# An encoder on one core: adds moved from Pool to VectorE, another start of an operand ring, and the times of four tiles

## The chip, the cores and the metric

The kernel runs on one core of a Trainium2 chip. The metric is device time in microseconds (us) for one execution. The core's engines each work through their own instructions in order: TensorE (PE in the profile, with PEld for its weight loads), VectorE (DVE), ScalarE (ACT), Pool (POOL, also called GpSimd) and SP, which only issues DMA transfers here. An engine that waits for a semaphore holds everything behind it on that engine.

## The reference

Two layers of an encoder over 1024 tokens of 1024 numbers, all in float32. Each layer adds a mixer and then a gated feed-forward block (FFN) to the stream:

```python
for l in range(DEPTH):                       # 2
    h = _rmsnorm(x, g_pre_mix[l])
    z = h @ w_in[l]                          # Fourier, windowed and memory groups
    ...
    x = x + _rmsnorm(y @ w_out[l], g_post_mix[l])   # y: the three groups, each normed
    h = _rmsnorm(x, g_pre_ffn[l])
    gate, up = jnp.split(h @ w_ffn_in[l], 2, axis=-1)
    f = (jax.nn.silu(gate) * up) @ w_ffn_out[l]     # D_FF = 2816
    x = x + _rmsnorm(f, g_post_ffn[l])
```

## The kernel before

**Tiles and precision.** The tokens are 8 tiles of 128 rows; tiles 0 to 3 are one half, 4 to 7 the other. Every float32 matmul is made from two rounded parts of each operand: `split` (L151, L152) writes the high part by a cast on ScalarE and the low part by a subtraction, mostly on VectorE, and three matmuls take hi*hi, hi*lo and lo*hi.

**The FFN.** Both FFN matrices are multiplied by a scheme with 7 products instead of 8 on 2 x 2 blocks. Each product takes sums or differences of blocks, so that there are many adds of 128 x 512 beside the matmuls.
- *Mixer to w_ffn_in.* `Mix.out` makes the mixer's output of a tile (eviction L1041), scales it and adds it to the stream (`residual`, L337 and L338), and norms it (`norm_x`, L294; its scale is computed in L210 and L212). `Blocks.tile` transposes the normed tile (L1066) and copies it to SBUF (L1067), and `Blocks.sum` and `Blocks.last` add the halves (L1084, L1096, L1097) into the operands that w_ffn_in's products share.
- *w_ffn_in.* `Quad.step` does the seven products of one block column in the order 2, 4, 5, 1, 6, 7, 3 (L1137). Its weights are loaded on SP (L1112), summed on VectorE (L1127) and split. 11 steps do all of gate and up. At the end of each, `up_out` multiplies (L1189), forms the sums that w_ffn_out's products need (L1199 to L1203) and writes them to `actd` in DRAM (L1193).
- *w_ffn_out.* `ffn_out` goes through the products 5, 3, 4, 1, 7, 2, 6 over 11 steps k. In each step `out_sums` loads an activation block from `actd` (L1233) and one or two weight blocks (L1239), adds these two (L1251; products 2 and 5 have none), on VectorE for even k and on Pool for odd k, and splits both into an operand of the ring `abs_`; 12 matmuls follow (L1270). At the end of a product the PSUM tiles are added into four result blocks (L1294 to L1309); for product 4 Pool does L1301.
- *The results of a tile.* `last_x` loads a tile of the stream (L1426), `last_tile` scales and adds: in layer 0 by `residual` (L337, L338) and back to DRAM (L1436), in layer 1 by `residual_out` (L327, L328) with half of the row stored from SP and half from ScalarE's queue (L329). Tiles 0 to 3 have their place inside the last two products, tiles 4 to 7 behind the last.

**Order and memory.** Nearly all buffers are places in one arena, handed out by rings, each with a list of slots that it goes round. Ring `abs_` is reset at each layer's w_ffn_out. The blocks of w_ffn_in's operands lie in slots too: block 2 in 64 and 72, block 4 in 80 and 88; `qws`, the raw weights, goes through 44, 48, 52, 56 from the second step. `zf_load`, for layer 1's mixer, writes its operands to slots 64 to 80 and is called behind product 1. The order of the instructions on each engine isn't that of the code: a scheduler with a model of the engines decides it when the program is built, so a change of one engine shifts others.

Of the kernel before, what the change touches and what calls it, by code (L numbers as in the profile page):

```python
# [16 lines left out]
ALU = mybir.AluOpType  # L17
# [5 lines left out]
NT = S // P  # L23
# [10 lines left out]
NFF = DFF // P  # L34
# [34 lines left out]
def tile_encoder(ctx: ExitStack, tc: tile.TileContext, T, C, out):  # L69
    nc = tc.nc  # L70
# [65 lines left out]
    wcs, abs_ = Ring(112, 116, 96, 100, 48, 52, 56, 60), Ring(80)  # L136
# [183 lines left out]
    def residual_out(x, f, g, dst, t):  # L320

        ss = sm(1, "rss")
        nc.scalar.activation(junks(D // 2).bitcast(BF16), f, AF.Square, accum_out=ss)
        r = rsqrt_mean(ss, D, 1, "rrs")
        for n in range(2):
            ns = slice(n * 512, n * 512 + 512)
            nc.vector.scalar_tensor_tensor(out=f[:, ns], in0=f[:, ns], scalar=r[:, 0:1], in1=g[:, ns], op0=ALU.mult, op1=ALU.mult)  # L327
            (nc.gpsimd if t in (1, 3, 5) else nc.vector).tensor_tensor(out=x[:, ns], in0=x[:, ns], in1=f[:, ns], op=ALU.add)  # L328
            (nc.sync, nc.scalar)[n].dma_start(dst[:, ns], x[:, ns])  # L329

    def residual(x, f, g, eng=None):
# [154 lines left out]
    class Mix:  # L486
# [543 lines left out]
        def out(self, t, x1):  # L1030

            x, f = self.xf.pop(t)
            (hi, lo), rs = self.prepped.pop(t)
            for n in range(2):
                ns = slice(n * 512, n * 512 + 512)
                pt = ps([512], "mo")
                acc = Acc(pt, 4)
                for i in range(4):
                    w = self.woa[2 + i]
                    acc.add(hi[:, i], lo[:, i], w[0][:, ns], w[1][:, ns])  # L1040
                nc.vector.scalar_tensor_tensor(  # L1041
                    out=f[:, ns], in0=pt, scalar=rs[:, 0:1], in1=f[:, ns], op0=ALU.mult, op1=ALU.add
                )
            residual(x, f, self.gpost, nc.gpsimd if t < NT - 1 else nc.vector)
            return norm_x(x, self.gffn, f, x1)


# [2 lines left out]
    class Blocks:  # L1050
# [18 lines left out]
        def sum(self, i, c, lo_eng=None):  # L1069

            b11, b21 = self.raw[0, 0], self.raw[0, 1]
            if i not in (2, 4):
                b12, b22 = self.raw[1, 0], self.raw[1, 1]
            sl = slice(c * P, c * P + P)
            if i not in self.b:
                self.b[i] = [big(4, 512) if k is None else at(k, 4, 512, dt=F32R) for k in self.HB[i]]
            if i == 2:
                s = b11[:, :, sl]
            if i == 5:
                s = b22[:, :, sl]  # L1080
            if i in (1, 4, 6):
                s = sums(4, P)
                x, y, op = (b21, b11, ALU.subtract) if i == 4 else (b11, b22 if i == 1 else b12, ALU.add)
                (nc.gpsimd if i == 6 else nc.vector).tensor_tensor(out=s, in0=x[:, :, sl], in1=y[:, :, sl], op=op)  # L1084
            if i == 7:
                s = b21[:, :, sl]
            if i == 3:
                s = b12[:, :, sl]
            hi, lo = (b[:, :, sl] for b in self.b[i])
            split(hi, lo, s, lo_eng)  # L1090

        def last(self, c):

            sl = slice(c * P, c * P + P)
            b12, b21, b22 = (self.raw[k][:, :, sl] for k in ((1, 0), (0, 1), (1, 1)))
            nc.gpsimd.tensor_tensor(out=b21, in0=b21, in1=b22, op=ALU.add)  # L1096
            nc.vector.tensor_tensor(out=b12, in0=b12, in1=b22, op=ALU.subtract)  # L1097

    ORDER = (2, 4, 5, 1, 6, 7, 3)
# [83 lines left out]

    def up_out(q, g, actd, p):

        V, G = nc.vector, nc.gpsimd
        a = [acts(512) for _ in range(4)]
        for i, c in enumerate(q.out):
            (G if i in (0, 3) else V).tensor_tensor(out=a[i], in0=c, in1=g[i], op=ALU.mult)  # L1189
        a11, a21, a12, a22 = a  # L1190

        def put(i, s):
            nc.sync.dma_start(actd[i - 1, p], s)  # L1193

        put(3, a11)
        put(4, a22)
        for i, x, y, eng in ((1, a11, a22, G), (2, a21, a22, V), (5, a11, a12, G)):
            s = acts(512)
            eng.tensor_tensor(out=s, in0=x, in1=y, op=ALU.add)  # L1199
            put(i, s)  # L1200
        V.tensor_tensor(out=a21, in0=a11, in1=a21, op=ALU.subtract)
        put(6, a21)
        G.tensor_tensor(out=a12, in0=a12, in1=a22, op=ALU.subtract)  # L1203
        put(7, a12)
# [24 lines left out]
    def out_sums(l, actd, i, k):  # L1229

        ab = abs_(2, 2, 512, dt=F32R)
        raw = ras(512)
        lastld[0] = nc.sync.dma_start(raw, actd[i - 1, k])  # L1233
        split(ab[:, 0, 0], ab[:, 0, 1], raw)

        def block(r, c):
            w = rbs(512)
            r0 = (2 * k + r) * P
            nc.sync.dma_start(w, T["w_ffn_out"][l, r0 : r0 + P, c * 512 : c * 512 + 512])  # L1239
            return w  # L1240

        if i in (2, 5):
            s = block(i == 5, i == 5)
        else:
            x, y, op = {
                4: ((1, 0), (0, 0), ALU.subtract), 3: ((0, 1), (1, 1), ALU.subtract), 1: ((0, 0), (1, 1), ALU.add),
                7: ((1, 0), (1, 1), ALU.add), 6: ((0, 0), (0, 1), ALU.add),
            }[i]
            x, y = block(*x), block(*y)
            s = bsums(512)  # L1250
            (nc.vector, nc.gpsimd)[k % 2].tensor_tensor(out=s, in0=x, in1=y, op=op)  # L1251
        split(ab[:, 1, 0], ab[:, 1, 1], s)
        return ab

    def ffn_out(l, actd, load, out, after, half, late):
# [16 lines left out]
        for i in (5, 3, 4, 1, 7, 2, 6):  # L1272
# [5 lines left out]
            for k in range(n):  # L1278
                ops.append(out_sums(l, actd, i, k))
                for p in range(whole):  # L1280
                    step(pts[p], p, ops[k], k == 0, k == n - 1, new)
                t = {(2, 2): 0, (2, 7): 1, (6, 1): 2, (6, 5): 3}.get((i, k))
                if t is not None:
                    load(t)
                    out(t, rows[t])
                if i == 6 and k in (7, 8, 9, 10):
                    load(k - 3)
            for p in range(4):
# [9 lines left out]
                    TT(out=c22[p], in0=pt, in1=c22[p], op=sub)  # L1298
                if i == 4:
                    nc.scalar.copy(c21[p], pt)  # L1300
                    nc.gpsimd.tensor_tensor(out=c11[p], in0=c21[p], in1=c11[p], op=sub)  # L1301
                if i == 1:
                    TT(out=c22[p], in0=pt, in1=c22[p], op=add)
                if i == 7:
# [53 lines left out]
    for l in range(DEPTH):  # L1358
# [69 lines left out]
        def last_tile(t, f):  # L1428
# [3 lines left out]
            if l == DEPTH - 1:  # L1432
                residual_out(x, f, st["gpf"], x_out[t], t)
                return
            residual(x, f, st["gpf"], nc.gpsimd if t < NT - 1 else None)
            nc.sync.dma_start(x2d[t], x)  # L1436
            token_scale(x, t)
            st[t] = x
# [2 lines left out]

        last = l + 1 == DEPTH
        abs_.i = 0
        abs_.ks = (64, 72, 80, 88, 16, 24, 0, 8, 32, 40, 48, 56, 96, 104, 112) if last else (80, 88, 48, 56, 96, 104)

        def after(i):
            if last:
                return
            if i == 5:
                mem.make()  # L1450
            if i == 1:
                mix.zf_load()
                mix.fourier_tables(28)
# [48 lines left out]
```

## Time and profile before

| | |
|---|---|
| times of three runs | 2122.41, 2131.86, 2132.92 us |
| median | 2131.86 us |
| the profiled execution | 2126.91 us |
| its span | 2125.1 us |
| granted TensorE clock, mean | 0.974 |
| TensorE busy | 2005.6 us (94%) |
| VectorE / ScalarE / Pool busy | 1572.2 / 1069.6 / 880.9 us |

The profile is that of one execution. Times in it start with the span; a row of the timeline has the start, the time to its end, the engine, the line, the operation, its output and inputs, their sizes, a count of like instructions put together, and in brackets how long the engine had been idle before and what released it. Layer 0's mixer ends at about 388 us, its w_ffn_in at about 837, its w_ffn_out at about 1050; layer 1's at about 1440, 1891 and the end.

### The profile page before, as it was taken

How to read it: one execution, taken by the hardware profiler on the slowest of the kernel's cores; microseconds unless marked ns; L12 is line 12 of the kernel's file. 1: busy time of each engine (PE TensorE's matmuls, PEld its weight loads, DVE VectorE, ACT ScalarE, POOL GpSimd, SP SyncE). 2: the span in 40 equal slices, each digit the busy share in tenths (PEclk: the TensorE clock that was granted, in tenths of full speed). 3: DMA queues.
4: the chain of work that ended last, by engine and by line, in shares of the span. 5: the costliest groups of instructions: out<-in, count | busy, mean ns of one | idle time of the engine just before them, and what ended most of it. 6: DMA issues, size and time to landing. Idle time of an engine off the chain costs nothing.

```text
span 2125.1 us, 28571 instructions
## 1 busy us (share of the span) xinstructions
PE 2005.6 (94%) x9587; PEld 1654.4 (78%) x9587; DVE 1572.2 (74%) x2429; ACT 1069.6 (50%) x2270; POOL 880.9 (41%) x922
## 2 busy tenths in 40 slices
PE   7998999699999999999899979996999999989997
PEld 6886877488888887788788768775888888878785
DVE  5668756897877877667847686679987787877774
ACT  7567777543333334454545676675433333345441
POOL 5344438533434335331634544574442333432222
PEclk9998999899999999999999989998999999999998
DMA  6112223422323326888821122142232232379882
GB/s 219 44 45 65 71 89 119 139 75 92 122 94 105 109 88 222 276 275 268 282 84 47 44 70 97 68 139 99 85 130 94 95 112 91 124 232 324 290 277 90
DMA packets 173347, 286.48 MB, mean 135 GB/s; under 512 B 15464, under 2 KB 73360, under 8 KB 173200
## 3 DMA queue, kind: packets, MB, share of 16 engines
q1 hardware_dynamic: 165136, 265.78, 38.0%
q10 hardware_dynamic: 8064, 18.88, 2.3%
q8 instruction: 75, 1.23, 0.2%
q14 instruction: 72, 0.59, 0.1%
HBM read 218.02 MB, written 66.58 MB: 134 GB/s over the span
## 4 chain that ended last, share of the span: by engine, by line
PE 75%; DVE 8%; DMA 5%; ACT 4%; POOL 4%; issue 3%; SPq 0%; POOLq 0%; DVEq 0%; ACTq 0%
PE fo L1270 14%; PE qy L1137 11%; PE qz L1137 11%; PE qx L1137 11%; PE mo L162 6%; PE qw L1137 5%; PE kvp L162 4%; DVE arena_r L152 3%; PE qp L162 3%; PE zT L162 2%; DMA arena_f<-in_w_ffn_out 2%; DMA arena_f<-actd 2%; PE pT L798 1%; ACT arena_r L151 1%; PE sc L761 1%
## 5 line engine op out<-in xcount | busy, mean ns | idle before, releaser
L151 ACT CAST arena_r<-arena_f 128x512 fp32r<-128x512 f32 (+2 forms) x780 | 443.3, 591 | 673.0 <-PE qz L1137 115.2
L152 DVE TENSOR_TENSOR arena_r<-arena_f,arena_r 128x512 fp32r<-128x512 f32 (+1 forms) x676 | 547.8, 832 | 174.3 <-ACT arena_r L151 172.2
L1270 PE MATMUL fo<-arena_r 128*128 128x512 f32 x1848 | 435.6, 397 | 27.3 <-ACT arena_r L151 15.2
L1270 PEld LDWEIGHTS fo<-arena_r 128*128 128x128 f32 x1848 | 353.3, 192 | 104.9 <-ACT arena_r L151 17.3
L1137 PE MATMUL qy<-arena_r 128*128 128x512 f32 x1056 | 262.3, 397 | 29.5 <-ACT arena_r L151 20.8
L1137 PEld LDWEIGHTS qy<-arena_r 128*128 128x128 f32 x1056 | 201.8, 192 | 73.8 <-ACT arena_r L151 21.5
L1127 DVE TENSOR_TENSOR arena_f<-arena_f 128x512 f32<-128x512 f32 x220 | 207.0, 943 | 5.1
L1157 POOL TENSOR_TENSOR arena_f<-arena_f 128x512 f32<-128x512 f32 x44 | 74.3, 1688 | 297.8 <-ACT arena_f L1142 295.4
L1137 PE MATMUL qz<-arena_r 128*128 128x512 f32 x704 | 196.0, 389 | 0.5 <-DVE arena_r L152 0.5
L1251 POOL TENSOR_TENSOR arena_f<-arena_f 128x512 f32<-128x512 f32 x50 | 72.0, 1441 | 217.9 <-DVE arena_r L152 154.1
L1137 PEld LDWEIGHTS qz<-arena_r 128*128 128x128 f32 x704 | 132.0, 188 | 28.4 <-DVE arena_r L152 1.0
L1189 POOL TENSOR_TENSOR arena_f<-arena_f 128x512 f32<-128x512 f32 x44 | 72.9, 1657 | 159.1 <-DVE arena_f L1169 125.5
L152 POOL TENSOR_TENSOR arena_r<-arena_f,arena_r 128x256 fp32r<-128x256 f32 (+2 forms) x104 | 83.1, 805 | 115.0 <-ACT arena_r L151 87.9
L1137 PE MATMUL qx<-arena_r 128*128 128x512 f32 x528 | 127.7, 389 | 0.5 <-ACT arena_r L151 0.5
L1137 PE MATMUL qw<-arena_r 128*128 128x512 f32 x528 | 127.8, 389 | 0.0
L1137 PE MATMUL qx<-big,arena_r 128*128 128x512 f32 x528 | 127.0, 389 | 0.0
L1137 PEld LDWEIGHTS qx<-arena_r 128*128 128x128 f32 x528 | 99.1, 188 | 21.4 <-ACT arena_r L151 0.9
L1137 PE MATMUL qz<-big,arena_r 128*128 128x512 f32 x352 | 115.5, 389 | 0.0
L1137 PEld LDWEIGHTS qw<-arena_r 128*128 128x128 f32 x528 | 99.1, 188 | 20.8 <-ACT arena_r L151 0.2
L1137 PEld LDWEIGHTS qx<-big,arena_r 128*128 128x128 f32 x528 | 99.1, 188 | 20.6
L162 PE MATMUL mo<-big,arena_r 128*128 128x512 f32 x384 | 104.1, 411 | 0.2 <-ACT arena_f L1001 0.2
L162 PE MATMUL qp<-big,arena_r 128*128 128x512 f32 x384 | 96.6, 400 | 4.7 <-POOL big L152 2.3
(228 smaller groups left out, 3567.5 us busy)
## 6 DMA issues: line engine op xcount, KB each, us to landing
arena_f<-in_w_ffn_out SPq DMA_DIRECT2D x264, 256.0 KB, 4.3
arena_f<-in_w_ffn_in SPq DMA_DIRECT2D x88, 512.0 KB, 3.6
actd<-arena_f SPq DMA_DIRECT2D x154, 256.0 KB, 3.6
arena_f<-actd SPq DMA_DIRECT2D x154, 256.0 KB, 4.3
arena_f<-in_w_in SPq DMA_DIRECT2D x40, 256.0 KB, 2.9
arena_f<-in_x SPq DMA_DIRECT2D x16, 512.0 KB, 4.4
arena_f<-in_w_out SPq DMA_DIRECT2D x32, 256.0 KB, 2.7
pmd<-arena_f ACTq DMA_DIRECT2D x32, 256.0 KB, 2.0
```

What stands on the lines that cost most here:

```text
L151: nc.scalar.copy(hi, src)
L152: return (lo_eng or nc.vector).tensor_tensor(out=lo, in0=src, in1=f32(hi), op=ALU.subtract)
L162: mm(self.dst, a, b, start=self.i == 0, stop=self.i == self.n - 1)
L761: mm(pt, lhs, self.kst[g][i][:, k0 * P : k1 * P], start=i == 0, stop=i == 1)
L798: nc.tensor.transpose(pT[:, h, :], es_[h // 2][:, h % 2, j * P : j * P + P], ident)
L1127: nc.vector.tensor_tensor(out=s, in0=a, in1=b, op=op)
L1137: mm(pt, a, b, start=start and n == 0, stop=n == 11, skip_group_check=not start)
L1157: nc.gpsimd.tensor_tensor(out=self.v, in0=self.v, in1=self.s2, op=ALU.add)
L1189: (G if i in (0, 3) else V).tensor_tensor(out=a[i], in0=c, in1=g[i], op=ALU.mult)
L1251: (nc.vector, nc.gpsimd)[k % 2].tensor_tensor(out=s, in0=x, in1=y, op=op)
L1270: mm(pt, ab[:, 0, x, sl], ab[:, 1, y], start=new and first and j == 0, stop=last and j == 2, skip_group_check=not new)
```

## The change

1. These adds go from Pool to VectorE: the residual add in `Mix.out` (L338, 14 instructions in both layers), the sum of operand 6 in `Blocks.sum` (L1084, 8), the first add of `Blocks.last` (L1096, 8), the five Pool operations of the last `up_out` of each layer (10), every second weight sum in `out_sums` (L1251, 50), the add of product 4 (L1301, 8), and the adds of FFN tiles 4 to 6 in layer 0 (L338, 3) and of tile 5 in layer 1 (L328, 2). These are 103 instructions. VectorE's TENSOR_TENSORs go from 1822 to 1925, Pool's from 571 to 468; matmuls and DMAs keep their numbers.
2. In layer 0 the operand ring of w_ffn_out begins with slots 64, 72, 80, 88 in place of 80, 88, 48, 56, and takes its former list after product 3.
3. Tiles 0 to 3 have their place in the sixth product (product 2, at k of 0, 2, 5 and 8). Before, two were there (k of 2 and 7) and two in the seventh.

```diff
@@ residual_out
-            (nc.gpsimd if t in (1, 3, 5) else nc.vector).tensor_tensor(out=x[:, ns], in0=x[:, ns], in1=f[:, ns], op=ALU.add)
+            (nc.gpsimd if t in (1, 3) else nc.vector).tensor_tensor(out=x[:, ns], in0=x[:, ns], in1=f[:, ns], op=ALU.add)
@@ Mix.out
-            residual(x, f, self.gpost, nc.gpsimd if t < NT - 1 else nc.vector)
+            residual(x, f, self.gpost)
@@ Blocks.sum
-                (nc.gpsimd if i == 6 else nc.vector).tensor_tensor(out=s, in0=x[:, :, sl], in1=y[:, :, sl], op=op)
+                nc.vector.tensor_tensor(out=s, in0=x[:, :, sl], in1=y[:, :, sl], op=op)
@@ Blocks.last
-            nc.gpsimd.tensor_tensor(out=b21, in0=b21, in1=b22, op=ALU.add)
+            nc.vector.tensor_tensor(out=b21, in0=b21, in1=b22, op=ALU.add)
@@ up_out
-        V, G = nc.vector, nc.gpsimd
+        V, G = nc.vector, nc.vector if p == NFF // 2 - 1 else nc.gpsimd
@@ out_sums
-            (nc.vector, nc.gpsimd)[k % 2].tensor_tensor(out=s, in0=x, in1=y, op=op)
+            nc.vector.tensor_tensor(out=s, in0=x, in1=y, op=op)
@@ ffn_out
-                t = {(2, 2): 0, (2, 7): 1, (6, 1): 2, (6, 5): 3}.get((i, k))
+                t = {(2, 0): 0, (2, 2): 1, (2, 5): 2, (2, 8): 3}.get((i, k))
...
-                    nc.gpsimd.tensor_tensor(out=c11[p], in0=c21[p], in1=c11[p], op=sub)
+                    TT(out=c11[p], in0=c21[p], in1=c11[p], op=sub)
@@ last_tile
-            residual(x, f, st["gpf"], nc.gpsimd if t < NT - 1 else None)
+            residual(x, f, st["gpf"], nc.gpsimd if t < 4 else None)
@@ behind last_tile
-        abs_.ks = (64, 72, 80, 88, 16, 24, 0, 8, 32, 40, 48, 56, 96, 104, 112) if last else (80, 88, 48, 56, 96, 104)
+        abs_.ks = (64, 72, 80, 88, 16, 24, 0, 8, 32, 40, 48, 56, 96, 104, 112) if last else (64, 72, 80, 88, 96, 104)
@@ after(i)
+            if i == 3:
+                abs_.ks = (80, 88, 48, 56, 96, 104)
```

**VectorE at layer 0's change from mixer to w_ffn_in.** `nrs` and `rrs` are the scales of a norm and of a residual, `mo` a mixer product, `big` the transposed halves. Before, from tile 5's norm (the first row) to ahead of the first weight sum L1127:

```order
L294 SCALAR_TENSOR_TENSOR arena_f<-arena_f,nrs_3943 128x1024
L960 TENSOR_SCALAR ms_3989<-ssp_3984 128x1
L337 SCALAR_TENSOR_TENSOR arena_f<-arena_f,rrs_4025 128x1024
L1084 TENSOR_TENSOR arena_f<-big_3545,big_4044 128x512
L152 TENSOR_TENSOR arena_r<-big_4044,arena_r 128x4x128
L1097 TENSOR_TENSOR big_4037<-big_4037,big_4044 128x4x128
L152 TENSOR_TENSOR arena_r<-arena_f,arena_r 128x4x128 x2
L1041 SCALAR_TENSOR_TENSOR arena_f<-mo_4066,grs_3991,arena_f 128x512
L1041 SCALAR_TENSOR_TENSOR arena_f<-mo_4080,grs_3991,arena_f 128x512
L1084 TENSOR_TENSOR arena_f<-big_3552,big_3545 128x512
L1084 TENSOR_TENSOR arena_f<-big_3545,big_4044 128x512
L152 TENSOR_TENSOR arena_r<-big_4044,arena_r 128x4x128
```

In the changed kernel the same norm is followed by one L1084 and tile 6's L337, and then by these rows, up to the first L1127:

```order
L1084 TENSOR_TENSOR arena_f<-big_3545,big_4044 128x512
L1096 TENSOR_TENSOR big_3552<-big_3552,big_4044 128x4x128
L1097 TENSOR_TENSOR big_4037<-big_4037,big_4044 128x4x128
L152 TENSOR_TENSOR arena_r<-arena_f,arena_r 128x4x128
L338 TENSOR_TENSOR arena_f<-arena_f 128x1024
L152 TENSOR_TENSOR arena_r<-big_4044,arena_r 128x4x128
L960 TENSOR_SCALAR ms_3989<-ssp_3984 128x1
L1084 TENSOR_TENSOR arena_f<-big_3545,big_4044 128x512
L1096 TENSOR_TENSOR big_3552<-big_3552,big_4044 128x4x128
L152 TENSOR_TENSOR arena_r<-arena_f,arena_r 128x4x128
L152 TENSOR_TENSOR arena_r<-big_4044,arena_r 128x4x128
L1127 TENSOR_TENSOR arena_f<-arena_f 128x512
```

Two L1096 and an L338 now stand on VectorE, the two evictions L1041 of the next tile are no longer ahead of L1127, and that comes fifteenth instead of fourteenth, counted from the norm.

**PE at layer 1's change from mixer to w_ffn_in.** `mo` are the mixer's output products, `hTp` the transposes of a normed tile, `qy` the first product of w_ffn_in. Before:

```order
L162 MATMUL mo_12473<-arena_r 128x512 x12
L958 MATMUL ssp_12450<-const,arena_f 128x2 x4
L162 MATMUL mo_12532<-arena_r 128x512 x12
L162 MATMUL mo_12546<-arena_r 128x512 x12
L1066 MATMUL hTp_12576<-const,arena_f 128x128 x4
L1066 MATMUL hTp_12582<-const,arena_f 128x128 x4
L1137 MATMUL qy_12602<-arena_r 128x512 x2
L1066 MATMUL hTp_12629<-const,arena_f 128x128 x4
```

With the change:

```order
L162 MATMUL mo_12532<-arena_r 128x512 x6
L162 MATMUL mo_12546<-arena_r 128x512 x6
L162 MATMUL mo_12532<-arena_r 128x512 x2
L162 MATMUL mo_12546<-arena_r 128x512 x2
L958 MATMUL ssp_12450<-const,arena_f 128x2 x2
L1066 MATMUL hTp_12576<-const,arena_f 128x128 x4
L1066 MATMUL hTp_12582<-const,arena_f 128x128 x2
L162 MATMUL mo_12532<-arena_r 128x512 x4
L162 MATMUL mo_12546<-arena_r 128x512 x4
L1066 MATMUL hTp_12582<-const,arena_f 128x128 x2
L1137 MATMUL qy_12602<-arena_r 128x512 x2
```

The transposes hTp_12576 and hTp_12582, which stood behind all mixer products, now stand between those of the last tile, with eight of these behind them.

**SP in the last product.** L1233 and L1239 load operands of w_ffn_out, L1426 loads tiles of the stream, L329 stores results. The last rows of SP before:

```order
L1239 DMA arena_f<-in_w_ffn_out 128x512
L1426 DMA arena_f<-x1d 128x1024
L329 DMA out<-arena_f 128x512 x2
L1233 DMA arena_f<-actd 128x512
L1426 DMA arena_f<-x1d 128x1024
L329 DMA out<-arena_f 128x512
L1233 DMA arena_f<-actd 128x512
L1426 DMA arena_f<-x1d 128x1024
L329 DMA out<-arena_f 128x512 x5
```

With the change:

```order
L1239 DMA arena_f<-in_w_ffn_out 128x512 x2
L1233 DMA arena_f<-actd 128x512
L1426 DMA arena_f<-x1d 128x1024
L329 DMA out<-arena_f 128x512 x3
L1239 DMA arena_f<-in_w_ffn_out 128x512 x2
L1233 DMA arena_f<-actd 128x512 x2
L1426 DMA arena_f<-x1d 128x1024 x2
L329 DMA out<-arena_f 128x512 x5
```

Before, the last operand load had three stores in the rows ahead of it, in two places, with a load of an operand between them; now three stores stand together, and two weight blocks and two activation blocks come behind them.

## The prediction

> **What bounds the kernel now.** The page comes first: the span, the busy times (its second line), and the chain that ended last by engine.
>
> ```profile
> span 2125.1 us, 28571 instructions
> PE 2005.6 (94%) x9587; PEld 1654.4 (78%) x9587; DVE 1572.2 (74%) x2429; ACT 1069.6 (50%) x2270; POOL 880.9 (41%) x922
> PE 75%; DVE 8%; DMA 5%; ACT 4%; POOL 4%; issue 3%; SPq 0%; POOLq 0%; DVEq 0%; ACTq 0%
> ```
>
> TensorE is busy for 94%. The change leaves its instructions as they are, so all there is to win is 2125.1 - 2005.6 = 119.5 us of idle time, and some matmuls at a lower clock. The table of windows shows where the idle time lies that the change can touch: start and end, length, then busy time of PE, PEld, DVE, ACT, POOL, granted clock, DMA share, GB/s. The last row is steady work.
>
> ```profile
> 384.00:424.00 40.00, 21.42 (x79) 15.90 (x77) 37.33 (x41) 20.76 (x39) 23.89 (x18) 0.74 0.42 139
> 836.00:880.00 44.00, 35.56 (x151) 27.93 (x150) 34.77 (x36) 21.41 (x40) 29.77 (x25) 0.92 0.91 307
> 1040.00:1052.00 12.00, 5.45 (x20) 3.84 (x19) 11.52 (x17) 6.40 (x12) 6.80 (x7) 0.84 0.81 264
> 1436.00:1476.00 40.00, 21.50 (x85) 16.63 (x84) 35.35 (x41) 20.68 (x37) 20.13 (x19) 0.74 0.39 132
> 1890.00:1898.00 8.00, 2.65 (x10) 1.88 (x9) 7.74 (x7) 2.33 (x5) 7.84 (x6) 0.79 0.77 229
> 2048.00:2084.00 36.00, 30.09 (x134) 24.64 (x132) 30.29 (x43) 14.62 (x26) 20.27 (x15) 0.98 0.81 274
> 900.00:1040.00 140.00, 140.00 (x626) 115.95 (x626) 102.45 (x138) 67.77 (x127) 46.09 (x40) 1.00 0.82 269
> ```
>
> Six places lose 18.6, 8.4, 6.5, 18.5, 5.4 and 5.9 us (length less PE): 63 in all. I call them A (mixer to w_ffn_in, layer 0), C (w_ffn_in to w_ffn_out, layer 0), D (end of w_ffn_out, layer 0), B (as A, layer 1), E (as C, layer 1) and G (last product). At A and B VectorE is the engine that is full (37.33 and 35.35 of 40) while the clock is at 0.74. Inside w_ffn_out PE never stops, and VectorE has 27% to spare (102.45 of 140).
>
> **A and B, the changes of stage.** What one add costs on either engine stands in the views by line: duration in ns as minimum/median/maximum.
>
> ```profile
> L1084 DVE TENSOR_TENSOR arena_f<-big,big x16: 676/686/1781, 340.6 to 1477.9; 128x512 f32<-128x512 f32 x16
> L1096 POOL TENSOR_TENSOR big<-big,big x8: 1280/1754/2244, 387.1 to 1475.6; 128x512 f32<-128x512 f32 x8
> L338 POOL TENSOR_TENSOR arena_f<-arena_f x14: 2335/2386/2821, 323.6 to 1443.1; 128x1024 f32<-128x1024 f32 x14
> L338 DVE TENSOR_TENSOR arena_f<-arena_f x2: 1210/1212/1214, 407.6 to 1454.6; 128x1024 f32<-128x1024 f32 x2
> ```
>
> An add is 0.69 us on VectorE against 1.28 on Pool (512 columns), and 1.21 against 2.39 (1024). But VectorE's 0.68 grows to 1.78 in its worst case, and Pool's 1.28 to 2.24: they slow each other. The timeline of A shows what that does.
>
> ```profile
> 383.90 1.28 DVE L294 SCALAR_TENSOR_TENSOR arena_f<-arena_f,nrs 128x1024 f32<-128x1024 f32 x1 [2.77 <-POOL nrs L212]
> 387.21 28.64 SPq L1112 DMA_DIRECT2D arena_f<-in_w_ffn_in  x7
> 390.40 2.83 DVE L1097 TENSOR_TENSOR big<-big,big 128x512 f32<-128x512 f32 x1
> 398.55 0.68 DVE L1127 TENSOR_TENSOR arena_f<-arena_f 128x512 f32<-128x512 f32 x1
> 400.13 1.22 PE L1137 MATMUL qy<-arena_r 128*128 128x512 f32 x2 [11.67 <-ACT arena_r L151]
> 407.76 4.63 PE L1137 MATMUL qy<-arena_r 128*128 128x512 f32 x10 [4.70 <-DVE arena_r L152]
> 415.38 2.48 DVE L152 TENSOR_TENSOR arena_r<-arena_f,arena_r 128x512 fp32r<-128x512 f32 x4
> ```
>
> PE stands for 11.67 us until the cast of the first weight sum (L1127), and for 4.70 more until the low part (L152). That L1127 ends at 399.23, 15.33 us after tile 5's norm (383.90) began; L1097 on the way takes 2.83. In the changed order VectorE has between the two the norm, a scaling and L338 (three of 1024 columns), eleven of 512 columns, and one of 0.15 (here 385.10 to 385.25): with 1.21 from the L338 row and 2.48 / 4 = 0.62 from the four subtractions in a row, 3 x 1.21 + 11 x 0.62 + 0.15 = 10.6. L1127 comes 4.7 us earlier: three adds come over from Pool, two mixer evictions now stand behind it, and nothing on Pool slows it. The low part now follows L1127 directly, so the second gap shrinks too. What is late next is the weights' load, issued at 387.21 with 3.6 to landing by the page's list, and ScalarE's casts. I take **A: -5** (-3.5 to -6).
>
> ```profile
> 1443.14 3.35 DVE L294 SCALAR_TENSOR_TENSOR arena_f<-arena_f,nrs 128x1024 f32<-128x1024 f32 x1 [0.44 <-POOL nrs L212]
> 1446.64 1.94 PE L1066 MATMUL hTp<-const,arena_f 128*128 128x128 f32 x8 [6.13 <-DVE arena_f L294]
> 1457.74 1.22 PE L1137 MATMUL qy<-arena_r 128*128 128x512 f32 x2 [9.15 <-ACT arena_r L151]
> 1466.45 5.05 PE L1137 MATMUL qy<-arena_r 128*128 128x512 f32 x14 [3.22 <-ACT arena_f L1142]
> ```
>
> At B the three gaps are 6.13, 9.15 and 3.22. The first hangs on a norm of 3.35 us where A's took 1.28: 2.1 us that go with Pool's add beside it. In the changed PE order tile 5's transposes stand between the last mixer products, so part of 6.13 is filled. Against it, VectorE has more nominal work between tiles 5 and 7 than it now spends, so the whole could also go to nothing. I take **B: -4** (-8 to 0).
>
> **C, D, E, the changes to and from w_ffn_out.** PE's first matmuls behind each gap:
>
> ```profile
> 842.06 19.03 PE L1270 MATMUL fo<-arena_r 128*128 128x512 f32 x72 [4.69 <-ACT arena_r L151]
> 1049.70 6.57 PE L1270 MATMUL fo<-arena_r 128*128 128x512 f32 x17 [4.80 <-DVE big L1307]
> 1896.74 3.78 PE L1270 MATMUL fo<-arena_r 128*128 128x512 f32 x8 [5.35 <-ACT arena_r L151]
> ```
>
> Layer 0's ring gets the first free buffers at C, as layer 1 has them already; yet layer 1 still loses 5.35 at E. So the ring's beginning is worth far less than C's 4.69: **C: -2** (-5 to 0), some of it from zf_load's operand writes, which now wait for the third product. That wait costs nothing as long as it lies ahead of the layer's end: two products later is 2 x 132 matmuls at 140.00 / 626 = 0.224, 59 us of cover. At D the eviction L1307 waits behind residual work; three residual adds leave Pool: **D: -1.5** (-4 to 0). At E five adds of the last up-projection leave Pool (7.84 of 8 busy): **E: -1** (-3 to 0).
>
> **G, and the four tiles.** The last product's timeline, and a window behind it:
>
> ```profile
> 2070.40 8.38 POOL L328 TENSOR_TENSOR arena_f<-arena_f,big 128x512 f32<-128x512 f32 x2 [3.83 <-DVE big L327]
> 2078.02 0.37 SPq L1233 DMA_DIRECT2D arena_f<-actd  x1
> 2078.74 1.25 POOL L1251 TENSOR_TENSOR arena_f<-arena_f 128x512 f32<-128x512 f32 x1
> 2083.93 6.33 PE L1270 MATMUL fo<-arena_r 128*128 128x512 f32 x16 [5.91 <-DVE big L1307]
> 2084.00:2087.40 3.40, 3.40 (x8) 2.71 (x9) 1.58 (x3) 0.00 (x0) 0.00 (x0) 0.50 0.08 31
> ```
>
> Tile 3's two Pool adds take 8.38 where two are worth 2.6: VectorE ran one two-input operation behind another. Its store holds SP, so the last load (2078.02) and Pool's last sum (2078.74) follow late, and PE stands 5.91 us, then runs at 0.50: 8 matmuls in 3.40, where 8 x 0.224 = 1.8, so 1.6 more. In the changed kernel the sum is VectorE's and the tiles come a product earlier, but SP's order still has three stores ahead of the last two loads, and tiles 1 and 3 stay on Pool. All of it would be 7.5; I take **G: -4** (-7.5 to 0).
>
> The Trainium skill, "SBUF — State Buffer", section "SBUF: two separate sides", calls the port pair that VectorE and Pool share an exclusive lock that one holds for a whole instruction and the other waits for. By that rule a Pool add waits for one VectorE operation, two take about 4 us, and G's share from this cause is nearer 3 than 7.5; the row's 8.38 speaks against it, so my 4 stands.
>
> For the clock, here is a shorter gap and what followed it.
>
> ```profile
> 2016.28 5.98 PE L1270 MATMUL fo<-arena_r 128*128 128x512 f32 x18 [2.81 <-ACT arena_r L151]
> 2017.50:2020.90 3.40, 3.40 (x9) 2.65 (x9) 3.40 (x7) 0.97 (x3) 0.00 (x0) 0.50 0.76 231
> ```
>
> A gap of 2.81 us was followed by 3.40 at 0.50 as well. So I count no clock won where a gap is shortened to 2 or 3 us. The Trainium skill, "TensorE: Matmul & The Clock Gate", section "Part 1: The HAM clock gate", lets the clock fall after an idle window of about 3.4 us; by that alone a G cut to 2 us would win 1.6 more. The trace disagrees.
>
> **What is added.** The 50 sums and 8 evictions in w_ffn_out go to VectorE:
>
> ```profile
> L1251 DVE TENSOR_TENSOR arena_f<-arena_f x60: 674/691/1753, 851.5 to 2075.1; 128x512 f32<-128x512 f32 x60
> L1251 POOL TENSOR_TENSOR arena_f<-arena_f x50: 1255/1298/1909, 859.8 to 2078.7; 128x512 f32<-128x512 f32 x50
> POOL arena_f L1251 <- DMA arena_f<-in_w_ffn_out: 50.4, 11, 9.6
> DVE arena_f L1251 <- DMA arena_f<-in_w_ffn_out: 16.5, 11, 5.0
> ```
>
> Per layer that is 29 x 0.69 = 20 us on an engine with 27% of some 200 us free, hidden behind PE. The other cost is the order: a sum at the head of VectorE's queue that waits for its block holds the splits and evictions behind it. The last two rows (total, times, longest) give this on Pool and on VectorE. All four tiles' loads and stores now lie in the sixth product, between its operands' loads on SP; a gap like the 2.81 above could open there. I take **+2**, between nothing and one such gap; the ends are 0 (there is no idle time inside the products for it to win) and +6 (two such gaps).
>
> **The sum.** -5 - 4 - 2 - 1.5 - 1 - 4 + 2 = -15.5. The profiled execution was 2126.91 for a span of 2125.1, 5 below the median of the three runs (2131.86, from 2122.41 to 2132.92). From its own time 2111.4; from the median, 2116. The ends are -33.5 and +2.5: 2098 to 2134.
>
> **The rivals.**
> 1. Both stage changes close further: weights' loads at B go out earlier too, A -8, B -8, C -5, D -2, E -1, G -6, nothing lost: -30, **2102**. For it: PE waits on VectorE's queue at both. Against it: at A the load and the casts come next. Chance 0.14.
> 2. The adds move, but the waits stay: VectorE, full at A and B, gets Pool's adds on top, so the time that no longer goes to slowed adds is filled again; G's stores still hold SP. A -3, B 0, C 0, D -1, E 0, G -2, +2: -4, **2128**. For it: VectorE's 37.33 of 40. Against it: the 15.33 against 10.6. Chance 0.27.
> 3. Slower: the sums wait at the head of VectorE's queue. An operand leads PE by at least one step of 12 matmuls, 2.7 us. If all eleven waits of 50.4 us move to VectorE as they are, 50.4 - 11 x 2.7 = 20.7 stops PE, and 11 times 1.6 at half clock adds 17.6; less 9 of A and B, +29: **2161**. It decides once blocks land more than 2.7 us behind their turn. Against it: VectorE's own sixty sums wait 16.5 us for the same queue, and PE doesn't stop. Chance 0.11.
>
> **How the numbers follow.** 0.5%, about what a measurement of this kernel can tell from no change, is 10.7 us. My forecast has 0.48: 0.42 below 2121, 0.06 above. Faster 0.42 + 0.14 = 0.56; same 0.06 + 0.27 = 0.33; slower 0.11. The range 2098 to 2131 holds the forecast, rival 1 and most of rival 2.
>
> **What would show it.** A: the first L1127 ends under 12 us behind tile 5's norm, and PE's 11.67 is 6 to 8. B: the norm is 1.3 and the first gap under 4. C: still a gap of 2 to 4. G: PE's gap is below 3, and no Pool add is over 3 us. Right in sum if PE's idle time falls by 12 to 20 us. Wrong if VectorE's waits on w_ffn_out blocks pass 50 us with new PE gaps inside w_ffn_out (rival 3), or if A and B still lose 17 us each (rival 2).

## The result, and the profile after

The changed kernel takes 2117.69 us (median of 6 runs, 2113.34 to 2118.48) against 2129.97 us before (median of 6): a ratio of 0.9941, interval 0.9927 to 0.9956. The change gains 12.3 us, 0.6%. The forecast was 2116.

The page's first lines: PE's share rises by one point, Pool loses 171 us of work (880.9 before), and VectorE's busy time stays (1572.2 before), although it does 103 more instructions.

```profile
span 2116.5 us, 28517 instructions
...
PE 2010.2 (95%) x9587; PEld 1658.1 (78%) x9587; DVE 1572.8 (74%) x2532; ACT 1069.3 (51%) x2270; POOL 710.2 (34%) x819
```

These are the windows at the same places of the program as the prediction's (columns as there): A, C, D, B, E, and the end of layer 1's sixth product.

```profile
387.40:427.40 40.00, 26.14 (x105) 20.05 (x103) 38.48 (x58) 23.08 (x43) 12.43 (x10) 0.79 0.36 119
834.00:878.00 44.00, 40.56 (x178) 32.91 (x178) 32.25 (x50) 24.44 (x45) 5.68 (x10) 0.96 0.89 314
1034.00:1046.00 12.00, 4.83 (x17) 3.67 (x16) 11.13 (x15) 7.07 (x14) 6.98 (x7) 0.74 0.90 296
1433.00:1473.00 40.00, 28.32 (x112) 21.68 (x111) 37.84 (x58) 22.53 (x43) 9.31 (x9) 0.83 0.35 113
1882.50:1890.50 8.00, 3.69 (x12) 2.65 (x11) 6.06 (x10) 1.24 (x2) 0.00 (x0) 0.74 0.97 291
2036.00:2072.00 36.00, 29.86 (x132) 24.40 (x130) 31.10 (x44) 14.30 (x27) 13.52 (x12) 0.98 0.81 266
```

At A, B and C PE is busier than before (21.42, 21.50 and 35.56), at D and at the end it is not. The last row ends inside a gap: PE starts again only at 2075.05, after 9.19 us without a matmul. At E, PE's idle time falls from 5.35 to 4.31. VectorE is as full at A and B as it was; it gets more done in the time. The views by line agree with that: with these adds all on VectorE they hardly stretch.

```profile
L1084 DVE TENSOR_TENSOR arena_f<-big,big x24: 678/686/693, 341.1 to 1463.0; 128x512 f32<-128x512 f32 x24
L1096 DVE TENSOR_TENSOR big<-big,big x8: 677/684/1230, 389.7 to 1463.6; 128x512 f32<-128x512 f32 x8
L338 DVE TENSOR_TENSOR arena_f<-arena_f x16: 1210/1218/1643, 327.1 to 1448.4; 128x1024 f32<-128x1024 f32 x16
```

L1084's longest is 0.69 us (1.78 before); the longest L1096 and L338 are still 1.23 and 1.64. In the timeline of A, L1127 ends at 396.43, 11.3 us after tile 5's norm began; before it was 15.33, and the forecast 10.6. PE's first gap is 5.25 us instead of 11.67:

```profile
385.13 1.28 DVE L294 SCALAR_TENSOR_TENSOR arena_f<-arena_f,nrs 128x1024 f32<-128x1024 f32 x1 [0.20 <-POOL nrs L212]
395.75 0.68 DVE L1127 TENSOR_TENSOR arena_f<-arena_f 128x512 f32<-128x512 f32 x1
397.14 1.22 PE L1137 MATMUL qy<-arena_r 128*128 128x512 f32 x2 [5.25 <-ACT arena_r L151]
400.74 1.97 PE L1066 MATMUL hTp<-const,arena_f 128*128 128x128 f32 x8 [2.38 <-DVE arena_f L294]
410.63 5.60 PE L1137 MATMUL qy<-arena_r 128*128 128x512 f32 x14 [4.51 <-ACT arena_f L1142]
```

At B two large gaps are left, 7.10 and 2.85 (6.13, 9.15 and 3.22 before):

```profile
1444.47 1.22 PE L1137 MATMUL qy<-arena_r 128*128 128x512 f32 x2 [7.10 <-ACT arena_r L151]
...
1455.43 5.09 PE L1137 MATMUL qy<-arena_r 128*128 128x512 f32 x14 [2.85 <-ACT arena_f L1142]
```

**Where the time went, stretch by stretch.** All matmuls are the same in every kernel here, so their count cuts the run into equal pieces of work. The table has the length of each piece in us, from the start times on PE in each trace (one execution each): the start (to the 1,200th instruction of PE, whose order is the same in all kernels), A (to the 2,100th: the rest of the mixer and the change to w_ffn_in), C (w_ffn_out's first 300 matmuls), the middle (its next 400), D (the rest, with the gap at its start), layer 1's mixer with B (to PE's 7,200th), E+F (w_ffn_out's first 700), and G (the rest). Both w_ffn_in are equal in all (401.4 and 331.6), as is the tail (8.5). D and G are the same place of the two layers, the change from the sixth to the seventh product: in the kernel before, layer 0's w_ffn_out goes on to 1084 us, and 1050 is the end of the gap behind its sixth product.

| kernel | median | start | A | C | middle | D | mixer 1 and B | E+F | G |
|---|---|---|---|---|---|---|---|---|---|
| before | 2129.97 | 244.8 | 188.3 | 93.4 | 91.7 | 64.8 | 469.9 | 171.2 | 59.6 |
| changed | 2117.69 | 248.8 | 182.0 | 87.1 | 91.7 | 64.6 | 471.0 | 166.7 | 63.1 |
| stage_alone | 2117.44 | 250.5 | 182.2 | 92.1 | 91.7 | 63.9 | 463.5 | 168.2 | 62.1 |
| stage_on_pool | 2121.38 | 245.4 | 188.3 | 86.6 | 91.7 | 64.5 | 472.7 | 168.5 | 63.0 |
| ring_as_before | 2112.39 | 245.9 | 181.4 | 91.9 | 91.7 | 64.9 | 458.8 | 166.8 | 62.9 |
| sums_on_pool | 2120.71 | 248.6 | 181.5 | 87.1 | 96.4 | 65.3 | 465.7 | 167.0 | 66.6 |
| tiles_alone | 2133.45 | 250.7 | 189.0 | 93.5 | 91.7 | 65.2 | 470.5 | 169.3 | 67.7 |
| tiles_as_before | 2097.37 | 247.0 | 182.0 | 87.8 | 91.7 | 60.8 | 460.9 | 165.5 | 58.5 |
| tiles_layer1_only | 2101.75 | 247.2 | 181.5 | 86.9 | 91.7 | 60.4 | 461.5 | 165.9 | 63.8 |
| no_pool_tiles | 2103.21 | 246.8 | 181.4 | 86.3 | 91.7 | 55.8 | 467.2 | 167.7 | 61.6 |
| no_pool_old_ring | 2104.56 | 248.6 | 181.9 | 92.8 | 91.7 | 55.9 | 460.9 | 166.9 | 62.4 |
| own_banks | 2093.22 | 252.9 | 181.8 | 87.3 | 91.7 | 55.7 | 466.8 | 165.6 | 50.9 |
| best | 2086.19 | 249.2 | 181.5 | 86.4 | 91.7 | 55.4 | 462.3 | 166.3 | 50.9 |
| best_old_ring | 2097.45 | 247.5 | 181.5 | 92.5 | 91.7 | 55.7 | 467.7 | 164.9 | 50.9 |

From before to changed: A -6.3, C -6.3, D -0.2, mixer and B +1.1, E+F -4.5, G +3.5. That is -12.7, against -12.3 between the medians; the spans differ by less (8.6) because the profiled execution of before had a start 4.0 us shorter, on the same instructions.

### The profile page after: what moved, and what is told of

The parts are those of the page before. It is cut to its first block, busy times and chain, and to the rows that moved or that the text cites. A ratio compares the mean times of both kernels' runs of the same rounds, so it can differ in the third digit from the quotient of the medians.

```text
span 2116.5 us, 28517 instructions
## 1 busy us (share of the span) xinstructions
PE 2010.2 (95%) x9587; PEld 1658.1 (78%) x9587; DVE 1572.8 (74%) x2532; ACT 1069.3 (51%) x2270; POOL 710.2 (34%) x819
## 3 DMA queue, kind: packets, MB, share of 16 engines
q8 instruction: 75, 1.23, 0.2%
## 4 chain that ended last, share of the span: by engine, by line
PE 77%; DVE 8%; DMA 6%; ACT 4%; issue 3%; POOL 2%; SPq 0%; DVEq 0%; ACTq 0%; POOLq 0%
PE fo L1270 14%; PE qy L1137 10%; PE qz L1137 10%; PE qx L1137 10%; PE mo L162 8%; PE qw L1137 5%; PE kvp L162 3%; PE qp L162 3%; DMA arena_f<-actd 3%; DVE arena_r L152 3%; PE zT L162 2%; PE pT L798 2%; PE sc L761 2%; ACT arena_r L151 1%; PE av L806 1%
## 5 line engine op out<-in xcount | busy, mean ns | idle before, releaser
L151 ACT CAST arena_r<-arena_f 128x512 fp32r<-128x512 f32 (+1 forms) x780 | 443.3, 591 | 651.5 <-PE qz L1137 118.3
L152 DVE TENSOR_TENSOR arena_r<-arena_f,arena_r 128x512 fp32r<-128x512 f32 (+1 forms) x676 | 504.9, 767 | 154.4 <-ACT arena_r L151 150.3
L1137 PE MATMUL qy<-arena_r 128*128 128x512 f32 x1056 | 263.9, 399 | 20.2 <-ACT arena_r L151 12.3
L1127 DVE TENSOR_TENSOR arena_f<-arena_f 128x512 f32<-128x512 f32 x220 | 206.2, 941 | 8.5 <-issue 2.4
L1157 POOL TENSOR_TENSOR arena_f<-arena_f 128x512 f32<-128x512 f32 x44 | 74.1, 1684 | 311.2 <-ACT arena_f L1142 311.2
L210 POOL TENSOR_SCALAR rrsv<-rss 128x1 f32<-128x1 f32 x32 | 11.4, 357 | 348.7 <-ACT arena_f L323 222.3
L1189 POOL TENSOR_TENSOR arena_f<-arena_f 128x512 f32<-128x512 f32 x40 | 66.8, 1671 | 159.5 <-DVE arena_f L1169 122.4
L162 PE MATMUL mo<-arena_r 128*128 128x512 f32 x384 | 101.9, 403 | 0.4 <-ACT arena_f L1001 0.3
```

What stands on the lines that cost most here:

```text
L151: nc.scalar.copy(hi, src)
L152: return (lo_eng or nc.vector).tensor_tensor(out=lo, in0=src, in1=f32(hi), op=ALU.subtract)
L162: mm(self.dst, a, b, start=self.i == 0, stop=self.i == self.n - 1)
L210: nc.gpsimd.tensor_scalar(out=v, in0=ss, scalar1=1.0 / n, scalar2=EPS, op0=ALU.mult, op1=ALU.add)
L1127: nc.vector.tensor_tensor(out=s, in0=a, in1=b, op=op)
L1137: mm(pt, a, b, start=start and n == 0, stop=n == 11, skip_group_check=not start)
```

## The experiments

Each kernel is the changed one with one more edit, unless it says otherwise. Ratios are to the kernel before.

**stage_on_pool.** The stage changes' adds go back:

```diff
-            residual(x, f, self.gpost)
+            residual(x, f, self.gpost, nc.gpsimd if t < NT - 1 else nc.vector)
...
-                nc.vector.tensor_tensor(out=s, in0=x[:, :, sl], in1=y[:, :, sl], op=op)
+                (nc.gpsimd if i == 6 else nc.vector).tensor_tensor(out=s, in0=x[:, :, sl], in1=y[:, :, sl], op=op)
...
-            nc.vector.tensor_tensor(out=b21, in0=b21, in1=b22, op=ALU.add)
+            nc.gpsimd.tensor_tensor(out=b21, in0=b21, in1=b22, op=ALU.add)
```

> The changed kernel with the adds of the two stage changes (Mix.out's L338, Blocks.sum's operand 6, Blocks.last's first add) back on Pool; the rest as changed. Theory (as predicted): VectorE's queue, slowed by Pool, bounds both stage changes; PE's gaps there, 13.9 us (A) and 10.6 us (B) with the change, go back to about 18 and 18.5, and the time rises from 2117.7 by about 12 to 2129. Rival (VectorE is full either way, the gain comes from w_ffn_out): gaps change by under 2 us each, the time stays within 2116 to 2121.

2121.38 us, ratio 0.9965 (0.9953 to 0.9977), 3.7 us over the changed kernel. At A the stretch is 188.3 us again, to the tenth what it was before, with the stretched L1097 and the full gap:

```profile
391.12 2.83 DVE L1097 TENSOR_TENSOR big<-big,big 128x512 f32<-128x512 f32 x1
399.27 0.68 DVE L1127 TENSOR_TENSOR arena_f<-arena_f 128x512 f32<-128x512 f32 x1
400.85 1.22 PE L1137 MATMUL qy<-arena_r 128*128 128x512 f32 x2 [11.67 <-ACT arena_r L151]
```

So A's 6.3 us come from these adds alone. The expected 12 didn't come: mixer 1 with B lost only 1.7 more than in the changed kernel, which had gained nothing there.

**stage_alone.** The same three edits the other way, made to the kernel before.

> The kernel before with only the adds of the two stage changes (Mix.out, Blocks.sum, Blocks.last) moved to VectorE. Theory (parts add up; taking them back from the changed kernel cost 3.7 us): PE's gaps at A go from 17.8 to about 14 and at B from 18.5 to 11 to 15, the time from 2129.9 to about 2126. Rival (the prediction's sizes for A and B, or more): 2121 or less.

2117.44, ratio 0.9947 (0.9933 to 0.9961): the rival's size. A gives 6.1 and mixer 1 with B 6.4. Alone, these three lines bring as much as the whole change, so that its other parts bring nothing in sum. Which of them takes, and which gives?

**ring_as_before.**

```diff
-        abs_.ks = (64, 72, 80, 88, 16, 24, 0, 8, 32, 40, 48, 56, 96, 104, 112) if last else (64, 72, 80, 88, 96, 104)
+        abs_.ks = (64, 72, 80, 88, 16, 24, 0, 8, 32, 40, 48, 56, 96, 104, 112) if last else (80, 88, 48, 56, 96, 104)
...
-            if i == 3:
-                abs_.ks = (80, 88, 48, 56, 96, 104)
```

> The changed kernel with layer 0's operand ring as before (slots 80, 88, 48, 56, 96, 104 from the start, no switch). The step ahead of w_ffn_out (C) lost 8.5 us of PE time before and 3.4 with the change. Theory (as predicted, the ring is worth about 2): C loses 5 to 6 us, time 2119 to 2121; the larger part of C's gain is then from the sums and the last up-projection on VectorE. Rival: the ring is what C's 5 us hang on; C loses 8 to 9 us again and the time is 2123 or more.

C is 4.8 us longer. PE stands 6.5 us there, in four gaps, between what the theory (5 to 6) and the rival (8 to 9) had:

```profile
834.82 19.52 PE L1270 MATMUL fo<-arena_r 128*128 128x512 f32 x72 [3.25 <-ACT arena_r L151]
855.61 8.45 PE L1270 MATMUL fo<-arena_r 128*128 128x512 f32 x36 [1.27 <-ACT arena_r L151]
865.24 2.12 PE L1270 MATMUL fo<-arena_r 128*128 128x512 f32 x8 [1.17 <-ACT arena_r L151]
...
869.93 3.02 PE L1270 MATMUL fo<-arena_r 128*128 128x512 f32 x12 [0.79 <-ACT big L1295]
```

Yet the time falls, to 2112.39, ratio 0.9919 (0.9906 to 0.9931): mixer 1 with B is 12.2 us shorter in this trace. Neither case had that. The ring isn't used there, but the scheduler gave the same instructions another order.

**sums_on_pool.**

```diff
-            nc.vector.tensor_tensor(out=s, in0=x, in1=y, op=op)
+            (nc.vector, nc.gpsimd)[k % 2].tensor_tensor(out=s, in0=x, in1=y, op=op)
...
-                    TT(out=c11[p], in0=c21[p], in1=c11[p], op=sub)
+                    nc.gpsimd.tensor_tensor(out=c11[p], in0=c21[p], in1=c11[p], op=sub)
```

> The changed kernel with every second weight sum L1251 and product 4's add L1301 back on Pool. Theory as predicted (the moved sums cost 2 us by VectorE's queue): 2115 to 2117, no gap comes back. Rival: the move of the sums is itself a gain (the gap of 2.81 us in layer 1's fifth product, part of C): 2120 to 2124, with gaps of 2 to 3 us inside w_ffn_out and more at C.

2120.71, ratio 0.9951 (0.9939 to 0.9963), 3.0 us over the changed kernel: the rival's time. Two gaps come or grow, both ended by evictions:

```profile
974.00 6.25 PE L1270 MATMUL fo<-arena_r 128*128 128x512 f32 x20 [3.12 <-DVE big L1303]
...
2079.39 5.82 PE L1270 MATMUL fo<-arena_r 128*128 128x512 f32 x17 [13.74 <-DVE big L1307]
```

The middle is 4.7 longer and G 3.5; mixer 1 with B is 5.3 shorter. C stays at 87.1, so the sums have no part in C's gain, and there the rival was wrong. The kernel before has the same adds on Pool, yet its middle is 91.7 and its G 59.6. So this run shows what the adds cost on Pool in the order that this kernel has, not what their move won against the kernel before.

**tiles_as_before**, **tiles_layer1_only** and **tiles_alone**: the times of tiles 0 to 3. The first has the former times in both layers, the second in layer 0 only; the third is the kernel before with only the new times.

```diff
-                t = {(2, 0): 0, (2, 2): 1, (2, 5): 2, (2, 8): 3}.get((i, k))
+                t = {(2, 2): 0, (2, 7): 1, (6, 1): 2, (6, 5): 3}.get((i, k))
```

> The changed kernel with tiles 0 to 3 at their former times (two in the sixth product, two in the seventh). Theory: four tiles' loads, scalings and stores packed into the sixth product are what raised the gap at its end (G) from 5.9 us to 9.2; with the former times G is 6 or less and the time 2112 to 2115. Rival: G hangs on the order on VectorE alone; it stays at 8 or more, the gap of 2.8 us in the fifth product returns or not, and the time is 2117 to 2121.

> The changed kernel with the former times of tiles 0 to 3 in layer 0 and the new ones in layer 1. Both former times gave 2097.4 against 2117.7. Theory: most of these 20 us lies in layer 0 (the end of w_ffn_out and the order that layer 1's mixer gets behind it), 4 to 5 at G: 2100 to 2104 here, with G at about 9. Rival: it is mainly layer 1's tiles: 2112 to 2117.

> The kernel before with only the times of tiles 0 to 3 moved into the sixth product, in both layers. Theory (packing the tiles there costs at the end of both w_ffn_out, D and G, whatever else is changed): D and G together lose 5 to 9 us more of PE time than before (6.6 and 5.9), the time is 2134 to 2139. The order of layer 1's mixer isn't touched in this kernel, so nothing is lost there. Rival (the times cost only in company of the other edits): 2126 to 2132.

2097.37 (0.9850, 0.9835 to 0.9866), 2101.75 (0.9878, 0.9860 to 0.9896) and 2133.45 (1.0023, 1.0010 to 1.0037). The first theory had the right sign and was too small: the new times cost 20 us in the changed kernel. About 4 lie at D, 4.6 at G and 10 in mixer 1 with B. With layer 0's times alone put back, G stays at 63.8 and the other two gains stand, so layer 0's tiles make 16 of the 20. Alone, the times cost 4.8; the theory's lower end, 2134, is just missed, and the cost lies at G only. There the trace has Pool's two adds at 8.94 us and a gap of 13.73 on PE:

```profile
2083.76 8.94 POOL L328 TENSOR_TENSOR arena_f<-arena_f,big 128x512 f32<-128x512 f32 x2 [2.55 <-DVE big L327]
...
2097.63 7.58 PE L1270 MATMUL fo<-arena_r 128*128 128x512 f32 x20 [13.73 <-DVE big L1307]
```

**no_pool_tiles.** No Pool adds are left in w_ffn_out's tiles:

```diff
-            (nc.gpsimd if t in (1, 3) else nc.vector).tensor_tensor(out=x[:, ns], in0=x[:, ns], in1=f[:, ns], op=ALU.add)
+            nc.vector.tensor_tensor(out=x[:, ns], in0=x[:, ns], in1=f[:, ns], op=ALU.add)
...
-            residual(x, f, st["gpf"], nc.gpsimd if t < 4 else None)
+            residual(x, f, st["gpf"])
```

> The changed kernel with the last Pool adds of w_ffn_out's tiles on VectorE too (tiles 0 to 3 of layer 0, tiles 1 and 3 of layer 1). With the change PE still stands 7.2 us at the end of layer 0's w_ffn_out (D) and 9.2 us at that of layer 1 (G). Theory: these hang on Pool's slowed adds (three L328 in 6.0 us), which hold the stores on SP and the last operands' loads behind them: G falls to 4 to 6, D to 4 to 6, the time to 2110 to 2113. Rival: they hang on the evictions L1307 standing behind sums and splits in VectorE's queue, whatever Pool does: the gaps stay or grow by the added 1.4 us, time 2117 to 2119.

2103.21, ratio 0.9877 (0.9864 to 0.9890), a larger gain than expected, but the theory held at one place of two, and there Pool's adds worked through the evictions, not through the stores. D fell by 8.8 us. In the changed kernel's trace a Pool add and a sum, both two-input operations, hit each other there; the sum's 0.69 became 2.83, ending half a microsecond behind Pool's, and the evictions L1307 stood behind it:

```profile
1037.14 2.72 POOL L338 TENSOR_TENSOR arena_f<-arena_f,big 128x1024 f32<-128x1024 f32 x1 [1.52 <-DVE big L337]
1037.58 2.83 DVE L1251 TENSOR_TENSOR arena_f<-arena_f 128x512 f32<-128x512 f32 x1
...
1042.36 12.29 PE L1270 MATMUL fo<-arena_r 128*128 128x512 f32 x44 [7.17 <-DVE big L1307]
```

This collision agrees with the exclusive port that the Trainium skill describes ("SBUF — State Buffer", section "SBUF: two separate sides"): VectorE waited until Pool's whole instruction was over. Beside two earlier Pool adds, two splits took 2.90 us (at 1016.59) and two sums 3.71 (at 1028.73), where two such operations take 1.28. Together the three collisions cost VectorE 6.2 us; that they make the gap is likely by the size, but the order there changed too. With the add on VectorE the gap is 0.44:

```profile
1032.32 9.55 PE L1270 MATMUL fo<-arena_r 128*128 128x512 f32 x41 [0.44 <-DVE big L1307]
```

At G the gap went from 9.19 only to 8.15, so there the rival holds: Pool's adds aren't what PE waits for in this kernel.

**own_banks.** no_pool_tiles, and in layer 1 the last product in PSUM banks of its own. Four more adds take the sixth product from the fourth block.

```diff
-            new = i in (5, 4, 1, 2)
+            new = i in (5, 4, 1, 2) or (i == 6 and late)
...
                 if i == 2:
                     TT(out=c21[p], in0=pt, in1=c21[p], op=add)
+                    if late:
+                        TT(out=c22[p], in0=c22[p], in1=pt, op=sub)
```

> The changed kernel with no Pool adds in w_ffn_out's tiles, and in layer 1 the last product in PSUM banks of its own (the sixth product is then subtracted from the fourth block by four more adds), so that its first matmuls needn't wait for the sixth product's evictions. Theory: G's 8.2 us hang on these evictions, which stand behind sums and splits on VectorE: G falls to 2 to 4, time from 2103.2 to 2096 to 2099. Rival: the operands of the last product are late as well: G stays at 6 or more, time 2101 to 2104.

2093.22, ratio 0.9828 (0.9810 to 0.9845), 10 us under no_pool_tiles. PE runs through the end of the sixth product without a stop, while the first eviction still starts 7.1 us behind that end (7.3 in no_pool_tiles):

```profile
2039.80 28.50 PE L1270 MATMUL fo<-arena_r 128*128 128x512 f32 x125
...
2062.94 0.68 DVE L1307 TENSOR_TENSOR big<-fo,big 128x512 f32<-128x512 f32 x1
```

So G's gap hangs on L1307 alone: the last product's first operands were ready. This is shown. The expected remainder of 2 to 4 us didn't come.

**no_pool_old_ring**: no_pool_tiles with ring_as_before's edit. **best**: no Pool adds in w_ffn_out's tiles, the former tile times, and the banks of own_banks. **best_old_ring**: best with ring_as_before's edit.

> The changed kernel with no Pool adds in w_ffn_out's tiles and the ring as before. If the ring's cost, 5.3 us, lies in layer 1's mixer and is independent of the tiles: 2103.2 - 5.3, 2096 to 2099, with 3 us more of gaps at C and 5 to 8 less between layer 0's w_ffn_out and layer 1's w_ffn_in. Rival: it was the order that the scheduler happened to give that kernel; with another order 2102 to 2106, C's 3 us worse and no gain in the mixer.

> What helped, together: the changed kernel with the former tile times, no Pool adds in w_ffn_out's tiles, and PSUM banks of its own for layer 1's last product. If the parts add up: from 2097.4 less the 5.8 us at G, 1.7 of half clock behind it and 2 to 4 at D: 2083 to 2089, with no gap at G. Rival (they overlap, or the order shifts again): 2091 to 2095.

> The kernel called best with layer 0's operand ring as before. If the ring is worth the 3 us that its absence cost at C in two kernels: 2 to 4 us over best, gaps at C of 6 to 7 us in place of about 4. Rival (it costs, as where it was taken from the changed kernel): 3 to 6 us under best.

2104.56 (0.9882, 0.9866 to 0.9898), 2086.19 (0.9791, 0.9772 to 0.9810) and 2097.45 (0.9846, 0.9825 to 0.9867). Only best came out as expected. The first has its rival's time, though its mixer did gain, and the last lost 11.3 us where 2 to 4 were expected. The former ring costs 6.5 and 6.1 us at C in these pairs, twice what was expected of it, beside 4.8 in the first. Mixer 1 with B moved by -6.3 and +5.4 with it, so once the ring's gain was hidden and once doubled. The first of these pairs has, all through mixer 1, the same two orders of instructions as the changed kernel and ring_as_before, where the difference was -12.2. So 5.9 us between the two pairs come from the executions and not from the order. best takes what each experiment pointed to; 42 us, 2.1%, under before, and 31.5 under the changed kernel. No gap is left at D (55.4 us) or G (50.9).

## Why the prediction was right, point by point

The time (2116 against 2117.7) and the first mechanism were right. Several terms were not, and they cancelled: against the table, C was 4.3 too small a gain, B with its mixer 5.1 and D 1.3 too large, and the rest 2.0 too large. That they nearly made up for each other is luck. Of the named signs, PE's idle time fell by 13.2 us (from 119.5 to 106.3; 12 to 20 were named), L1127 at A came at 11.3, and C's gaps are 3.4. But G's gap is 9.19 where less than 3 was named, and B's first is 7.10 where less than 4 was.

- **A, -5; measured -6.3.** Right, and shown by stage_on_pool and stage_alone: VectorE's queue, slowed by Pool, was the bound.
- **B, -4; measured +1.1 with the mixer ahead of it.** B itself was right: cut at PE's 6,760th instruction, behind which the work is the same, it took 120.2 us before and 116.6 after, with 18.5 and 13.4 us of idle time. The mixer ahead gave it back, with 349.7 before and 354.4 after. stage_alone, with the same adds, has -6.4 in both together. The changed kernel's order of mixer 1 is a poor one; it comes with layer 0's new tile times (4 to 10 us, see below), which the prediction didn't price at all.
- **C, -2; measured -6.3.** The step that failed is the one from E to C: layer 1 has the first free buffers already and yet loses 5.35 at E, so the ring should be worth far less than C's 4.69. The ring's beginning is worth 4.8 to 6.5 in three pairs; E's wait is another one. A gap of like size at a like place proved nothing about its cause.
- **D, -1.5; measured -0.2.** The prediction counted three adds that leave Pool and not the four that stay, which now collide with sums on VectorE.
- **E, -1, the moved sums, +2, and G, -4, together -3; measured -1.0.** E+F gained 4.5, and G gave 3.5 back. E's gap fell by 1.0, as forecast. A cost of the moved sums doesn't show: put back on Pool, they lose 4.7 in the middle and 3.5 at G (sums_on_pool). But the kernel before had them on Pool without these losses, so their share of the 12.3 us stays open. The waits for weight blocks didn't move over as the slower rival feared, 24.5 us now against 16.5 and Pool's 50.4 before:

```profile
DVE arena_f L1251 <- DMA arena_f<-in_w_ffn_out: 24.5, 21, 4.2
```

The sign of G was wrong too. The prediction saw the stores on SP and Pool's adds ahead of the last loads, took them for the cause, and credited the earlier tiles. In the changed kernel's timeline the chain is all there, but it ends in VectorE's queue:

```profile
2056.98 6.03 POOL L328 TENSOR_TENSOR arena_f<-arena_f,big 128x512 f32<-128x512 f32 x3
2059.65 3.73 SPq L329 DMA_DIRECT2D out<-arena_f  x3
2065.90 0.93 SPq L1233 DMA_DIRECT2D arena_f<-actd  x2
2071.21 3.09 DVE L152 TENSOR_TENSOR arena_r<-arena_f,arena_r 128x512 fp32r<-128x512 f32 x5
2074.22 2.47 DVE L1307 TENSOR_TENSOR big<-fo,big 128x512 f32<-128x512 f32 x4
2075.05 15.25 PE L1270 MATMUL fo<-arena_r 128*128 128x512 f32 x54 [9.19 <-DVE big L1307]
```

PE needs only the evictions. The scheduler had put them behind all of the last product's sums and splits: none comes after the first eviction, though PE takes another 33 us over that product. The loads of its last two activation blocks go out only from 2065.90 on, when the sixth product has just ended (2065.86). Whatever delays these (a store, a slow add, four tiles in one product) delays PE. An F that ends earlier only makes PE arrive earlier at that queue: in stage_alone, whose order there is that of before, E+F is 3.0 shorter and G 2.5 longer.
- **The rivals.** The second (adds move, waits stay) is out at A, and right in that G's stores still held SP. At B with its mixer (0) and at D (-1) it was nearer than the forecast. The first was nearer at C (-5), and wrong at B (-8). The third didn't occur.
- **The order of mixer 1.** With the stage adds on VectorE, mixer 1 with B is short in six kernels (458.8 to 463.5) and long in five (465.7 to 471.0). This goes by the order of its instructions. In the changed kernel, no_pool_tiles and own_banks every engine has the same order there (471.0, 467.2 and 466.8). A second order is common to tiles_as_before, tiles_layer1_only and best (460.9, 461.5 and 462.3), a third to ring_as_before and no_pool_old_ring (458.8 and 460.9). So the ring, layer 0's tile times and the sums change the order, the first two with either sign, and the adds of the tiles leave it alone. Within one order the length still differs by up to 4.2 us: the same 2,256 matmuls kept PE busy for 438.8 us in the changed kernel and 431.4 in no_pool_tiles, at a mean granted clock of 0.96 and 0.97. So 4 to 10 us of the changed kernel's loss is its order. Why that order is the longer one stays open.

## What to carry to other kernels

Where two engines slow each other's two-input operations and one's queue is the bound, the other is better left out there, as at A; taking only half of the adds away left collisions at D. Ask of a gap which instruction it waits for and what stands ahead of that in its queue: an eviction that frees a bank shouldn't queue behind prefetched work, and a bank of its own removed a wait of 8 us that no faster add had. Where a scheduler sets the order, one edit's time includes a reshuffle elsewhere; cut the run at equal counts of matmuls to see which part is the edit's, and compare the orders before calling the rest a reshuffle: one order alone differed by 4 us between traces.

## What the runs showed of the hardware

The first 1,200 instructions of PE, in the same order in all fourteen kernels, took from 244.8 to 252.9 us. The windows of the shortest and the longest, before and own_banks, show it in the granted clock:

```profile
0.00:240.00 240.00, 214.13 (x1177) 182.53 (x1177) 163.82 (x336) 159.25 (x388) 108.75 (x179) 0.96 0.27 86
```

```profile
0.00:240.00 240.00, 212.14 (x1133) 180.71 (x1134) 158.87 (x322) 153.06 (x372) 107.20 (x178) 0.91 0.26 85
```

That is 8 us, 0.4% of the run, from the same work at 0.96 and 0.91; 2 of them are idle time. The Trainium skill, "TensorE: Matmul & The Clock Gate", section "Part 1: The HAM clock gate", says that the gate's window runs free of the kernel's start, so that the same kernel falls into it differently. The traces agree in so far as the same order was granted different clocks; the window itself no run here shows. And a Pool add beside a busy VectorE isn't held up by one instruction only: two took 8.94 us in tiles_alone and 8.38 before, one of them 7.72 and 7.14, where the shortest take 1.26 and 1.27.
